# Seven products of half blocks in place of eight in the feed-forward's second projection

## The chip, the cores and the metric

The kernel runs on one core of one Trainium2 chip. The core has a matrix engine (TensorE, PE in the profile, with its weight loads shown apart as PEld), a vector engine (DVE), a scalar engine (ACT), a general engine (POOL) and a sync engine (SP) that here issues the loads. Working memory is SBUF, with 128 partitions; PE writes its sums to PSUM, which has eight banks of 128 x 512 floats. The metric is the time of one execution on the device, in microseconds (us); lower is better.

## The reference

A two-layer encoder over 512 tokens of 1024 features. Each layer mixes tokens (differential attention beside a bidirectional gated recurrence), projects the result and adds it to x, and then has a gated feed-forward with 2816 hidden features, which is the part that matters here:

```python
h = rmsnorm(x, ffn_norm[layer])
x = x + (jax.nn.silu(h @ w_gate[layer]) * (h @ w_up[layer])) @ w_down[layer]
```

All arrays are float32. `w_gate` and `w_up` are 1024 x 2816 for each layer. After the second layer comes one more normalisation.

## The kernel before

**Layout.** Activations are kept with features on the partitions: `xT` has 8 chunks of 128 features by 512 tokens. `hh` and `hl` are the two parts of `xT` times the gain of the norm: `hh` is the value rounded to the type that PE multiplies at full rate (fp32r), `hl` the rest. The norm's factor per token, `rbc`, is multiplied in after the projection, when a result leaves PSUM.

**A product in three matmuls.** Weights are split in the same way (`wsplit`, L196, by `split_act`, L91: ACT casts the high part, DVE subtracts it to get the low part), and `mm3` (L207) multiplies high by high, high by low, and low by high into one sum. One tile of 128 hidden features is 8 chunks x 3 matmuls of 128 x 128 weights by 512 tokens.

**The feed-forward loop** (L838 to L859). The 22 tiles of hidden features go in 11 pairs. For each pair one load each brings 1024 x 256 weights of `w_gate` and of `w_up` into a raw buffer (`wload`, L188; pool `wraw`, two buffers, issued on the SP queue). For each of the two tiles the gate's half of the columns is split and multiplied, then the up's half. The gate's sum is multiplied by `rbc` on DVE and goes through Silu on ACT; the up's sum is multiplied by `rbc`; their product is split into `gh` and `gl` (22 tiles by 512 tokens each), the operands of the projection by `w_down` that follows.

**Buffers.** Split weights have three pairs of buffers (`wsplit`, each 1024 elements of high part and of low part on a partition). Sums use four banks (`mbank`), and four more (`bank`) serve other work. Results in progress (`gu`) have two buffers for the gate and two for the up.

**Order.** The kernel is written in a tile framework that gives each engine its own list of instructions in order and puts the waits in. Work under `urgent()` goes ahead of other work that is ready at the same time: the loads, the splits, and all that takes a sum out of PSUM. Matmuls have normal priority and keep the order of the program as far as their operands are ready. A buffer is given to the next tile when all readers of the one in it are done.

Of the kernel before, what the change touches and what calls it, by code (L numbers as in the profile page):

```python
# [9 lines left out]
F32 = mybir.dt.float32  # L10
F32R = mybir.dt.float32r
I32 = mybir.dt.int32
I8 = mybir.dt.int8
AF = mybir.ActivationFunctionType
ALU = mybir.AluOpType
# [3 lines left out]
P = 128  # L19
D = 1024  # L20
DC = D // P
T = 512
# [4 lines left out]
FC = FFN // P  # L27
# [20 lines left out]
def kernel(  # L48
# [17 lines left out]
    PE, DVE, ACT, POOL = nc.tensor, nc.vector, nc.scalar, nc.gpsimd  # L66
    load = nc.sync.dma_start
    urgent = tc.high_priority

    def act(o, i, func, bias=None, scale=None, accum=None):  # L70
        kw = {}
        if bias is not None:
            kw["bias"] = bias
        if scale is not None:
            kw["scale"] = scale
        if accum is not None:
            kw["accum_out"] = accum
        return ACT.activation(o, i, func, **kw)  # L78

    def tt(o, a, b, op):  # L80
        return DVE.tensor_tensor(o, a, b, op)  # L81

    def stt(o, a, s, b, op0, op1):
        return DVE.scalar_tensor_tensor(o, a, s, b, op0, op1)
# [6 lines left out]
    def split_act(src, hi, lo):  # L91
        return ACT.copy(hi, src), tt(lo, src, hi.bitcast(F32), ALU.subtract)  # L92
# [9 lines left out]
    hp = ctx.enter_context(tc.tile_pool(name="wsplit", bufs=3))  # L102
# [4 lines left out]
    def bank(name="s"):  # L107
        return pside.tile([P, T], F32, tag="s", name=name)

    def mbank(name="m"):  # L110
        return pm.tile([P, T], F32, tag="m", name=name)
# [31 lines left out]
    xT = cp.tile([P, DC, T], F32, name="xT")  # L143
    hh = cp.tile([P, DC, T], F32R, tag="hh", name="hh")
    hl = cp.tile([P, DC, T], F32R, tag="hl", name="hl")
    rbc = cp.tile([P, T], F32, name="rbc")
# [41 lines left out]
    def wload(src):  # L188

        _, k, c = src.shape  # L190
        raw = wp.tile([P, 2048], F32, tag="raw", name="raw")
        v = raw[:, :k * c].rearrange("p (k c) -> p k c", c=c)
        load(v, src)
        return v

    def wsplit(v):  # L196

        _, k, c = v.shape
        hi = hp.tile([P, 1024], F32R, tag="hi", name="hi")[:, :k * c].rearrange("p (k c) -> p k c", c=c)
        lo = hp.tile([P, 1024], F32R, tag="lo", name="lo")[:, :k * c].rearrange("p (k c) -> p k c", c=c)  # L200
        split_act(v, hi, lo)
        return hi, lo

    def rows(w, k0, nk, c0, n):
        return w[k0 * P:(k0 + nk) * P, c0:c0 + n].rearrange("(k p) c -> p k c", p=P)

    def mm3(ps, lh, ll, rh, rl, start, stop):  # L207
        PE.matmul(ps, lh, rh, start=start, stop=False)  # L208
        PE.matmul(ps, lh, rl, start=False, stop=False)  # L209
        PE.matmul(ps, ll, rh, start=False, stop=stop)  # L210
# [44 lines left out]
    for j in range(5):  # L255
        b = 1 << j
        m = masks[:, j, :]
# [10 lines left out]
    with tc.tile_pool(name="init", bufs=1, reuse_waits="tile") as ip:  # L268
# [4 lines left out]
        with urgent():  # L273
            ACT.dma_start(vecs, small)
            for c in range(DC):
                if c % 4 == 0:
                    raw = wp.tile([P, 2048], F32, tag="raw", name="raw").rearrange("p (k d c) -> p k d c", k=4, d=2)
                src = w_in[0][c * P:(c + 1) * P, B_FF:B_FF + 2 * 512].rearrange("p (d c) -> p d c", d=2)[:, :, 0:2 * P]
# [7 lines left out]
        first = [mbank(), mbank(), bank("m"), bank("m")]  # L286
        for c in range(DC):
            with urgent():
                if c % 2 == 0:
                    hi, lo = [hp.tile([P, 1024], F32R, tag=tag, name=tag).rearrange("p (k d c) -> p k d c", k=2, d=2)  # L290
                              for tag in ("hi", "lo")]
                wh, wl = hi[:, c % 2], lo[:, c % 2]
# [17 lines left out]
        with tc.issue_after(norms[-1][1].ins):  # L310
# [53 lines left out]
            for dst, quarter in ((sin, 0.0), (cos, 0.25)):  # L364
                n = ip.tile([P, 32], F32, tag="n", name="n")
# [361 lines left out]
    last_silu = None  # L727
    for l in range(LAYERS):
        win = w_in[l]
        an = [vecs[:, V_FFN + 8 * l + c:V_FFN + 8 * l + c + 1] for c in range(DC)]  # L730
        with ExitStack() as mix:
# [59 lines left out]
            with tc.tile_pool(name=f"merge{l}", bufs=1, reuse_waits="tile") as gm, ExitStack() as late:  # L791
# [11 lines left out]
                with tc.tile_pool(name=f"attn{l}", bufs=1, reuse_waits="tile") as ap:  # L803
# [6 lines left out]
                               k=4, ah=obh, al=obl)  # L810
# [24 lines left out]
        with tc.tile_pool(name=f"ffn{l}", bufs=2, reuse_waits="tile") as fp:  # L835
            gh = fp.tile([P, FC, T], F32R, name="gh", bufs=1)
            gl = fp.tile([P, FC, T], F32R, name="gl", bufs=1)
            for f0 in range(0, FC, 2):  # L838
                with urgent():
                    rg = wload(rows(w_gate[l], 0, DC, f0 * P, 256))  # L840
                    ru = wload(rows(w_up[l], 0, DC, f0 * P, 256))
                for f in (f0, f0 + 1):
                    c0 = slice((f - f0) * P, (f - f0 + 1) * P)
                    tmp = []
                    for raw in (rg, ru):
                        with urgent():
                            wh, wl = wsplit(raw[:, :, c0])
                        ps = mbank()
                        for c in range(DC):
                            mm3(ps, wh[:, c, :], wl[:, c, :], hh[:, c, :], hl[:, c, :], c == 0, c == DC - 1)  # L850
                        s = fp.tile([P, T], F32, tag=f"gu{len(tmp)}", name="gu")
                        with urgent():
                            tt(s, ps, rbc, ALU.mult)
                            if not tmp:
                                last_silu = act(s, s, AF.Silu)
                        tmp.append(s)
                    with urgent():
                        tt(tmp[0], tmp[0], tmp[1], ALU.mult)
                        split_act(tmp[0], gh[:, f, :], gl[:, f, :])  # L859
            with tc.issue_after(last_silu.ins):  # L860
                lnexp = ACT.preload_act_table_set("natural_log_exp_and_others")
            groups = [(0, 8), (8, 8), (16, 6)]
            if l < LAYERS - 1:
                nn = [vecs[:, V_ATT + 8 * (l + 1) + c:V_ATT + 8 * (l + 1) + c + 1] for c in range(DC)]
                for c0 in range(0, DC, 2):
                    ps = [mbank(), mbank()]
                    for k0, nk in groups:
                        with urgent():
                            raw = wload(rows(w_down[l], k0, nk, c0 * P, 256))
                        for j in range(2):  # L870
                            with urgent():
                                wh, wl = wsplit(raw[:, :, j * P:(j + 1) * P])
                            for k in range(nk):
                                f = k0 + k
# [8 lines left out]
            else:  # L883
# [10 lines left out]
                ps = [[mbank(), mbank()] if t < 2 else [bank(), bank()] for t in range(TC)]  # L894
# [5 lines left out]
                for k, t, c0, n in order:  # L900
                    if k not in sp:
                        with urgent():
                            if k % 2 == 0:
                                raw = wload(rows(w_down[l], k, 2, 0, D))
                            sp[k] = wsplit(raw[:, k % 2:k % 2 + 1, :])
                    wh, wl = sp[k]
# [3 lines left out]
                for t in range(TC):  # L910
                    last = t == TC - 1
                    ss = sm.tile([P, 4], F32, tag="fss", name="fss")
                    v = [xt[:, t, c0:c0 + n] for c0, n in pieces[t]]
# [58 lines left out]
```

## Time and profile before

| | us |
|---|---|
| median of 3 runs | 1620.51 |
| lowest, highest | 1620.45, 1620.62 |
| the profiled execution | 1621.18 |
| its span, first to last instruction | 1619.2 |
| gate and up projections of layer 0, about | 452.3 to 691.2 |
| gate and up projections of layer 1, about | 1252 to 1491 |

In rows of groups the columns are the line of the kernel, the engine, the operation, out<-in by the program's names (`m` is a main bank, `s` a side bank), shapes, count, busy time, mean duration in ns, and the idle time of the engine before, with what ended it. In a timeline the first two numbers are start and duration. In rows by stage come the stretch, its length, then busy time and count of PE, weight loads, DVE, ACT and POOL, the granted clock of PE, the DMA share and GB/s. Durations of matmuls overlap, since they are pipelined and their ends are modelled, so the cost of one is read from the step between starts.

### The profile page before, as it was taken

Reading aid. Unit: us, or ns where it says so; the run is one execution under the profiler, and the core shown is the slowest. Engines: PE = TensorE matmul, PEld = TensorE weight load, DVE = VectorE, ACT = ScalarE, POOL = GpSimd, SP = SyncE. Lnnn points to the kernel's source line nnn. Section 1 sums busy time; section 2 is a strip of 40 time slices with the busy share of each in tenths; the row PEclk is TensorE's granted clock in tenths of the full one; section 3 lists DMA queues with packets and bytes.
Section 4 is the critical chain, followed back from the end, with each engine's and each line's share of the span. In section 5 each row is a group of like instructions: output and inputs, shape, how many; then the busy total and the mean of one; then the engine's idle time right before and its main releaser. Section 6 shows DMA issues by size and latency. Waiting matters only on the chain.

```text
span 1619.2 us, 18754 instructions
## 1 busy us (share of the span) xinstructions
PE 1604.5 (99%) x7473; PEld 1325.0 (82%) x7473; DVE 1013.5 (63%) x1637; ACT 772.0 (48%) x1188; POOL 9.1 (1%) x21
## 2 busy tenths in 40 slices
PE   9999999999999999999999999999999999999998
PEld 7888888887888888888888888888878888888886
DVE  8888877887654444433368789688875444444224
ACT  4666666676433323322355667676754323233213
POOL 2000000000000000000000000000000000000000
PEclk9999999999999999999999999999999999999999
DMA  6212212221333222323322222122123233332321
GB/s 206 88 58 73 79 57 75 78 79 53 104 104 98 85 87 95 114 90 100 102 91 83 74 78 79 54 77 79 52 79 100 83 104 104 105 103 93 104 82 74
DMA packets 118071, 142.53 MB, mean 88 GB/s; under 512 B 3168, under 2 KB 100704, under 8 KB 117984
## 3 DMA queue, kind: packets, MB, share of 16 engines
q1 hardware_dynamic: 117696, 141.05, 26.7%
q8 instruction: 58, 0.95, 0.2%
q10 hardware_dynamic: 288, 0.30, 0.1%
q14 instruction: 29, 0.24, 0.0%
HBM read 139.23 MB, written 2.10 MB: 87 GB/s over the span
## 4 chain that ended last, share of the span: by engine, by line
PE 85%; DVE 9%; ACT 4%; issue 1%; DMA 0%; SPq 0%; DVEq 0%; ACTq 0%
PE m L209 24%; PE m L210 24%; PE m L208 24%; DVE fl L81 2%; DVE lo L81 2%; PE sc L549 1%; PE s L208 1%; PE s L209 1%; PE s L210 1%; PE qk L666 1%; ACT hi L92 1%; DVE z L81 1%; PE wt L718 1%; PE po L600 1%; PE qk L663 1%
## 5 line engine op out<-in xcount | busy, mean ns | idle before, releaser
L92 ACT CAST hi<-raw 128x1024 fp32r<-128x1024 f32 (+2 forms) x274 | 272.4, 995 | 610.0 <-PE m L209 477.5
L208 PE MATMUL m<-hh,hi 128*128 128x512 f32 x1216 | 475.1, 391 | 0.9 <-ACT hh L78 0.5
L210 PE MATMUL m<-hh,lo 128*128 128x512 f32 x1216 | 475.4, 391 | 0.0
L209 PE MATMUL m<-hl,hi 128*128 128x512 f32 x1216 | 474.7, 390 | 0.0
L81 DVE TENSOR_TENSOR lo<-raw,hi 128x1024 fp32r<-128x1024 f32 (+2 forms) x282 | 321.0, 1139 | 182.7 <-ACT hi L92 181.8
L208 PEld LDWEIGHTS m<-hh,hi 128*128 128x128 f32 x1216 | 228.3, 188 | 47.9 <-ACT hh L78 1.0
L210 PEld LDWEIGHTS m<-hh,lo 128*128 128x128 f32 x1216 | 228.3, 188 | 47.6 <-DVE lo L81 0.7
L209 PEld LDWEIGHTS m<-hl,hi 128*128 128x128 f32 x1216 | 228.4, 188 | 47.0
L81 DVE TENSOR_TENSOR gu<-m,rbc 128x512 f32<-128x512 f32 x88 | 60.9, 692 | 241.3 <-PE m L210 237.3
L208 PE MATMUL m<-hi,hh 128*128 128x512 f32 x256 | 101.4, 396 | 0.0
L209 PE MATMUL m<-lo,hh 128*128 128x512 f32 x256 | 100.8, 394 | 0.0
L210 PE MATMUL m<-hi,hl 128*128 128x512 f32 x256 | 100.8, 394 | 0.0
L78 ACT ACTIVATE fl<-fl 128x1024 f32<-128x1024 f32 (+1 forms) x56 | 48.5, 873 | 44.8 <-DVE fl L81 44.8
L208 PE MATMUL m<-gh,hi 128*128 128x512 f32 x176 | 68.5, 389 | 0.0
L209 PE MATMUL m<-gl,hi 128*128 128x512 f32 x176 | 68.5, 389 | 0.0
L210 PE MATMUL m<-gh,lo 128*128 128x512 f32 x176 | 68.5, 389 | 0.0
L210 PEld LDWEIGHTS m<-hi,hl 128*128 128x128 f32 x256 | 48.1, 188 | 9.5
L209 PEld LDWEIGHTS m<-lo,hh 128*128 128x128 f32 x256 | 48.2, 188 | 9.3
L208 PEld LDWEIGHTS m<-hi,hh 128*128 128x128 f32 x256 | 48.2, 188 | 9.3
L549 PEld LDWEIGHTS sc<-fl 128*128 128x128 f32 x384 | 49.1, 191 | 7.9 <-issue 3.2
L549 PE MATMUL sc<-fl 128*128 128x128 f32 x384 | 51.3, 276 | 2.3 <-DVE fl L81 2.2
L208 PE MATMUL m<-mh,hi 128*128 128x512 f32 x128 | 49.4, 391 | 1.0 <-ACT hi L92 1.0
(258 smaller groups left out, 2353.9 us busy)
## 6 DMA issues: line engine op xcount, KB each, us to landing
raw<-in_w_in_dram SPq DMA_DIRECT2D x46, 1024.0 KB, 5.0
raw<-in_w_gate_dram SPq DMA_DIRECT2D x22, 1024.0 KB, 5.1
raw<-in_w_up_dram SPq DMA_DIRECT2D x22, 1024.0 KB, 5.1
raw<-in_w_down_dram SPq DMA_DIRECT2D x19, 1024.0 KB, 4.8
raw<-in_w_o_dram SPq DMA_DIRECT2D x8, 1024.0 KB, 4.7
raw<-in_w_b_dram SPq DMA_DIRECT2D x4, 1024.0 KB, 4.9
raw<-in_w_a_dram SPq DMA_DIRECT2D x4, 1024.0 KB, 5.0
raw<-in_w_down_dram SPq DMA_DIRECT2D x4, 768.0 KB, 4.1
```

Source lines behind the costliest of these rows:

```text
L78: return ACT.activation(o, i, func, **kw)
L81: return DVE.tensor_tensor(o, a, b, op)
L92: return ACT.copy(hi, src), tt(lo, src, hi.bitcast(F32), ALU.subtract)
L208: PE.matmul(ps, lh, rh, start=start, stop=False)
L209: PE.matmul(ps, lh, rl, start=False, stop=False)
L210: PE.matmul(ps, ll, rh, start=False, stop=stop)
L549: mm = PE.matmul(ps[:, c], K[:, c], Q[:, c], start=True, stop=True)
L600: mm = PE.matmul(po[:, tok], a, b, start=i == 0, stop=i == len(terms) - 1)
L663: mm = PE.matmul(ps[c], q2[:, c, tok], ka[:, c, :], start=True, stop=False)
L666: PE.matmul(ps[c], q2[:, c, tok], kb[:, c, :], start=False, stop=True)
L718: tr = PE.transpose(pt[:, s * P:(s + 1) * P], w[:, 0, s * P:(s + 1) * P], ident)
```

## The change

For the seven pairs of tiles 4 to 17 the up projection of a pair is computed as one 2 x 2 block product. The weights of the pair are cut into blocks by tile (i) and by even and odd chunks of the 1024 input features (j), a_ij; the activations by even and odd chunks and by halves of the tokens, x_jh. The usual way needs eight products of blocks; the new one (Winograd's form of Strassen's scheme) needs seven, of sums and differences of blocks. Each product is 4 chunks x 3 matmuls of 128 x 128 weights by 256 tokens. Gate tiles stay as they were, and so do the pairs of tiles 0 to 3 and 18 to 21, apart from the shape of their buffers.

- `combine(k)` makes the four mixed copies of the activations once for each layer, for one pair of chunks at a time: with the norm's gains, x12 - x11, x22 - x12 + x11, x22 - x12, and x21 - x22 + x12 - x11, each split into two parts. Four calls stand among the first four tiles. Two of the copies lie in the part of `gh` and `gl` for the last four tiles, which isn't filled until the end, and two in new tiles (`own`).
- `seven(rg, ru, f0)` makes the sums of weight blocks on DVE (two scratch tiles, and in place in the raw buffer), splits them into four sets of split buffers (`first` to `fourth`), runs the products between the two gate tiles, and puts the results together on DVE from three side banks and one main bank. `rbc` is multiplied into the gates' results, which are then multiplied with the ups', for both tiles in one instruction each.
- The results of a pair are now one tile of 2 x 512 for the gates and one for the ups, with a single buffer each.

```diff
         with tc.tile_pool(name=f"ffn{l}", bufs=2, reuse_waits="tile") as fp:
             gh = fp.tile([P, FC, T], F32R, name="gh", bufs=1)
             gl = fp.tile([P, FC, T], F32R, name="gl", bufs=1)
+            own = [fp.tile([P, DC // 2, 2, T // 2], F32R, name=name, bufs=1) for name in ("comh", "coml")]
+            half = lambda v: v.rearrange("p (h t) -> p h t", h=2)
+            spare = [v[:, FC - 4:FC, :].rearrange("p k (h t) -> p k h t", h=2) for v in (gh, gl)]
+            com = lambda part, i, k: (spare if i < 2 else own)[part][:, k, i % 2, :]
+
+            def combine(k):
+                ge, go = an[2 * k], an[2 * k + 1]
+                (x11, x12), (x21, x22) = [[half(xT[:, c, :])[:, i, :] for i in range(2)] for c in (2 * k, 2 * k + 1)]
+                d, e = [half(fp.tile([P, T], F32, tag=tag, name="com", bufs=1)) for tag in ("s1", "s2")]
+                u, v, m, n = d[:, 0, :], d[:, 1, :], e[:, 0, :], e[:, 1, :]
+                tt(u, x12, x11, ALU.subtract)
+                act(u, u, AF.Copy, scale=ge)
+                stt(m, x22, go, u, ALU.mult, ALU.subtract)
+                act(v, x12, AF.Copy, scale=ge)
+                stt(v, x22, go, v, ALU.mult, ALU.subtract)
+                stt(n, x21, go, m, ALU.mult, ALU.subtract)
+                for i, src in enumerate((u, m, v, n)):
+                    split_act(src, com(0, i, k), com(1, i, k))
+
+            def pair_of(tag):
+                return fp.tile([P, 2, T], F32, tag=tag, name="gu", bufs=1)
...
+            def gate(s, raw):
+                ps = tile_of(raw)
+                with urgent():
+                    tt(s, ps, rbc, ALU.mult)
+                    return act(s, s, AF.Silu)
+
+            def seven(rg, ru, f0):
+                s, u = pair_of("gu0"), pair_of("gu1")
+                quarter = u.rearrange("p f (h t) -> p (f h) t", h=2)
+                blk = lambda i, j: ru.rearrange("p (k two) c -> p k two c", two=2)[:, :, j, i * P:(i + 1) * P]
+                a11, a12, a21, a22 = blk(0, 0), blk(0, 1), blk(1, 0), blk(1, 1)
...
+                gate(s[:, 0, :], rg[:, :, 0:P])
+                with urgent():
+                    first = wsplit(ru[:, :, 0:P])
+                    second = two()
+                    tt(s1, a21, a22, ALU.add)
+                    tt(s2, s1, a11, ALU.subtract)
+                    split_act(s2, second[0][:, 0], second[1][:, 0])
+                    tt(a21, a11, a21, ALU.subtract)
+                    split_act(a21, second[0][:, 1], second[1][:, 1])
+                p1 = mbank()[:, :T // 2]
+                b26, b57, b34 = [half(bank("y")) for _ in range(3)]
+                product(p1, lambda part, k: first[part][:, 2 * k, :], plain(0, 0))
+                with urgent():
+                    ACT.copy(quarter[:, 1, :], p1)
+                product(b26[:, 0, :], lambda part, k: first[part][:, 2 * k + 1, :], plain(1, 0))
+                with urgent():
+                    third = two()
+                    split_act(s1, third[0][:, 0], third[1][:, 0])
+                    split_act(a22, third[0][:, 1], third[1][:, 1])
+                product(b26[:, 1, :], of(second, 0), mixed(1))
+                with urgent():
+                    tt(quarter[:, 0::3, :], quarter[:, 1:2, :].to_broadcast([P, 2, T // 2]), b26, ALU.add)
+                    tt(s2, a12, s2, ALU.subtract)
+                    fourth = two()
+                    split_act(s2, fourth[0][:, 0], fourth[1][:, 0])
+                product(b57[:, 1, :], of(second, 1), mixed(2))
+                product(b57[:, 0, :], of(third, 0), mixed(0))
+                with urgent():
+                    tt(quarter[:, 1:3, :], quarter[:, 3:4, :].to_broadcast([P, 2, T // 2]), b57, ALU.add)
+                    tt(quarter[:, 3, :], quarter[:, 2, :], b57[:, 0, :], ALU.add)
+                product(b34[:, 1, :], of(third, 1), mixed(3))
+                product(b34[:, 0, :], of(fourth, 0), plain(1, 1))
+                with urgent():
+                    tt(quarter[:, 1:3, :], quarter[:, 1:3, :], b34, ALU.add)
+                silu = gate(s[:, 1, :], rg[:, :, P:2 * P])
+                with urgent():
+                    tt(s, s, rbc.unsqueeze(1).to_broadcast([P, 2, T]), ALU.mult)
+                    tt(u, u, s, ALU.mult)
+                    split_act(u, gh[:, f0:f0 + 2, :], gl[:, f0:f0 + 2, :])
+                return silu
+
             for f0 in range(0, FC, 2):
                 with urgent():
                     rg = wload(rows(w_gate[l], 0, DC, f0 * P, 256))
                     ru = wload(rows(w_up[l], 0, DC, f0 * P, 256))
...
+                if 4 <= f0 < FC - 4:
+                    last_silu = seven(rg, ru, f0)
+                    continue
+                s, u = pair_of("gu0"), pair_of("gu1")
+                for i in range(2):
+                    if f0 + i < DC // 2:
+                        combine(f0 + i)
+                    last_silu = gate(s[:, i, :], rg[:, :, i * P:(i + 1) * P])
+                    ps = tile_of(ru[:, :, i * P:(i + 1) * P])
...
```

More of the change, by code (lines that the diff above doesn't have):

```diff
@@ new lines, in pair_of, with tile_of @@
+            def pair_of(tag):
+                return fp.tile([P, 2, T], F32, tag=tag, name="gu", bufs=1)
+            def tile_of(raw):
+                with urgent():
+                    wh, wl = wsplit(raw)
+                ps = mbank()
+                for c in range(DC):
+                    mm3(ps, wh[:, c, :], wl[:, c, :], hh[:, c, :], hl[:, c, :], c == 0, c == DC - 1)
+                return ps
+            def gate(s, raw):
[3 more added lines that the diff above has]
+                    return act(s, s, AF.Silu)
@@ new lines, in seven, with two, product @@
+            def seven(rg, ru, f0):
[3 more added lines that the diff above has]
+                a11, a12, a21, a22 = blk(0, 0), blk(0, 1), blk(1, 0), blk(1, 1)
+                s1, s2 = [fp.tile([P, T], F32, tag=tag, name="sw", bufs=1).rearrange("p (k c) -> p k c", c=P)
+                          for tag in ("s1", "s2")]
+                def two():
+                    return [hp.tile([P, 1024], F32R, tag=tag, name=tag).rearrange("p (h k c) -> p h k c", h=2, c=P)
+                            for tag in ("hi", "lo")]
+                def product(ps, w, right):
+                    for k in range(DC // 2):
+                        mm3(ps, w(0, k), w(1, k), right(0, k), right(1, k), k == 0, k == DC // 2 - 1)
+                plain = lambda odd, h: lambda part, k: half((hh, hl)[part][:, 2 * k + odd, :])[:, h, :]
+                mixed = lambda i: lambda part, k: com(part, i, k)
+                of = lambda v, h: lambda part, k: v[part][:, h, k, :]
+                gate(s[:, 0, :], rg[:, :, 0:P])
[33 more added lines that the diff above has]
+                silu = gate(s[:, 1, :], rg[:, :, P:2 * P])
+                with urgent():
+                    tt(s, s, rbc.unsqueeze(1).to_broadcast([P, 2, T]), ALU.mult)
+                    tt(u, u, s, ALU.mult)
+                    split_act(u, gh[:, f0:f0 + 2, :], gl[:, f0:f0 + 2, :])
+                return silu
@@ L841 @@
                     ru = wload(rows(w_up[l], 0, DC, f0 * P, 256))
[L842 to L856, printed above, removed]
+                if 4 <= f0 < FC - 4:
[7 more added lines that the diff above has]
+                    ps = tile_of(ru[:, :, i * P:(i + 1) * P])
                     with urgent():
-                        tt(tmp[0], tmp[0], tmp[1], ALU.mult)
-                        split_act(tmp[0], gh[:, f, :], gl[:, f, :])
+                        tt(u[:, i, :], ps, rbc, ALU.mult)
+                        tt(u[:, i, :], u[:, i, :], s[:, i, :], ALU.mult)
+                        split_act(u[:, i, :], gh[:, f0 + i, :], gl[:, f0 + i, :])
             with tc.issue_after(last_silu.ins):
```

## The prediction

> **What bounds the kernel now.** I read the page's busy shares and chain of waits first, then the busy times by stage, then inside the stage that the change touches the groups and the timeline.
>
> ```profile
> span 1619.2 us, 18754 instructions
> PE 1604.5 (99%) x7473; PEld 1325.0 (82%) x7473; DVE 1013.5 (63%) x1637; ACT 772.0 (48%) x1188; POOL 9.1 (1%) x21
> ...
> PE 85%; DVE 9%; ACT 4%; issue 1%; DMA 0%; SPq 0%; DVEq 0%; ACTq 0%
> ```
>
> TensorE is busy all through and carries 85% of the chain that ended last. By stage (length, then busy times of PE, weight loads, DVE, ACT):
>
> ```profile
> 0.00:446.00 446.00, 439.75 (x2123) 362.25 (x2124) 361.06 (x680) 276.09 (x455) 9.08 (x21) 1.00 0.26 86
> 452.30:495.82 43.52, 43.51 (x192) 35.56 (x192) 20.39 (x25) 16.09 (x20) 0.00 (x0) 1.00 0.30 96
> 495.82:691.20 195.38, 195.38 (x864) 161.83 (x863) 90.23 (x108) 60.26 (x73) 0.00 (x0) 1.00 0.32 101
> 1252.00:1491.00 239.00, 238.99 (x1066) 197.77 (x1065) 110.47 (x133) 77.18 (x95) 0.00 (x0) 1.00 0.32 103
> ```
>
> The second and third rows are the gate and up projections of layer 0 (first two pairs of feature tiles, then the other nine), the last those of layer 1. PE is without a gap in them, at clock 1.00, with DVE at 46% and ACT at 32%: here time is the number of matmuls by their spacing, and nothing else.
>
> The spacing comes from starts in the timeline, since the durations of matmuls overlap:
>
> ```profile
> 469.73 0.39 PE L208 MATMUL m<-hh,hi 128*128 128x512 f32 x1
> ...
> 475.17 0.39 PE L208 MATMUL m<-hh,hi 128*128 128x512 f32 x1
> ...
> 1610.41 0.28 PE L208 MATMUL s<-hi,gh 128*128 128x256 f32 x1
> ...
> 1612.44 0.28 PE L210 MATMUL s<-hi,gl 128*128 128x256 f32 x1
> ```
>
> The first two rows are 24 matmuls apart, one tile of 128 features: 5.44 us, 0.2267 us for each 512 columns. The last two stand at the ends of the kernel's only 18 matmuls of 256 columns (the last tile of tokens): 17 steps in 2.03 us, 0.1194 us each. So half the columns cost 0.527 of the time, not half.
>
> **The change, part by part.**
>
> *Products on PE.* For a pair of feature tiles the two up tiles take 2 x 8 x 3 = 48 matmuls of 512 columns: 48 x 0.2267 = 10.88 us. The new form has seven products of 4 chunks x 3 matmuls, 84 of 256 columns: 84 x 0.1194 = 10.03 us. With both gate tiles a pair goes from 21.76 to 20.91 us: 0.85 us less, of which eight-to-seven would give 1.36 and the dearer half width takes 0.51 back. Seven pairs in two layers: 14 x 0.85 = **11.9 us**. The start times are read to 0.01 us, so the spacing is good to about 0.0012 us, or 1.4 us in the sum.
>
> Each half-width matmul brings a full weight load, whose record is longer than the new spacing:
>
> ```profile
> L210 PEld LDWEIGHTS s<-hi,gl 128*128 128x128 f32 x5 | 1.0, 192 | 0.0
> ```
>
> Since each of the 18 matmuls had its own load, loads too came every 0.119 us; the 0.192 us is latency that overlaps. The Trainium skill, "TensorE: Matmul & The Clock Gate", "What overlaps and what doesn't", says that a load overlaps a running matmul only when it goes to another row group. By that, and with its figure of about 107 ns for 128 columns, a half-width step would be an estimated 0.107 + 0.107 = 0.21 us, and the 84 matmuls would take 17.9 us in place of 10.88. The trace disagrees: full-array loads came 0.119 us apart.
>
> *Work on DVE and ACT.* The rows for the pieces (columns: busy us, mean ns, idle before):
>
> ```profile
> L81 DVE TENSOR_TENSOR lo<-raw,hi 128x1024 fp32r<-128x1024 f32 x44 | 53.8, 1222 | 4.8 <-ACT hi L92 4.8
> L92 ACT CAST hi<-raw 128x1024 fp32r<-128x1024 f32 x44 | 46.4, 1054 | 146.8 <-PE m L209 144.2 <-issue 2.5
> L81 DVE TENSOR_TENSOR gu<-m,rbc 128x512 f32<-128x512 f32 x44 | 30.4, 692 | 120.8 <-PE m L210 118.8 <-ACT rbc L78 2.0
> L78 ACT ACTIVATE gu<-gu 128x512 f32<-128x512 f32 x22 | 13.9, 634 | 0.0
> L92 ACT CAST gh<-gu 128x512 fp32r<-128x512 f32 x22 | 13.7, 625 | 14.2 <-DVE gu L81 14.2
> ...
> L81 DVE TENSOR_TENSOR xt<-xt,s 128x256 f32<-128x256 f32 x2 | 0.8, 417 | 0.7 <-PE s L210 0.7
> L78 ACT ACTIVATE sqf<-xt 128x256 f32<-128x256 f32 x2 | 0.8, 409 | 0.8 <-DVE xt L81 0.8
> L84 DVE SCALAR_TENSOR_TENSOR xt<-xt,fss,fng 128x256 f32<-128x256 f32 x2 | 0.9, 480 | 0.6 <-ACT fss L78 0.6
> ```
>
> Before, a pair costs DVE 4 x 1.22 (low parts of weights) + 8 x 0.69 (evacuations, products, low parts of results) = 10.4 us. After: six operations of 1024 elements (three low parts of whole tiles, the scaling of both gates, the product, the low part of the result), fourteen of 512 (two gate evacuations, four sums of weight blocks, five low parts of them, three evacuations) and one of 256: 6 x 1.22 + 14 x 0.69 + 0.42 = **17.4 us of 20.91**, 83%. ACT goes to 4 x 1.05 + 5 x 0.62 + 2 x 0.63 + 0.41 = 9.0 us. Strided weight blocks I take at the same price, since the present split reads 128 of every 256 columns already. All of this lies beside PE as long as it is in time; without that cover it would be 7 us of DVE per pair.
>
> *Is it in time?* Count from the start of a pair's first gate tile. PE does that gate until 5.44, products 1 to 7 until 6.87, 8.30, 9.74, 11.17, 12.60, 14.04 and 15.47, the second gate until 20.91. There are three buffers of split weights, taken in turn by gate, first, second, third, fourth, gate. The third is free at 5.44 and wanted at 11.17, the fourth free at 8.30 and wanted at 14.04, the second gate free at 11.17 and wanted at 15.47, the next pair's gate free at 14.04 and wanted at 20.91, its first product free at 15.47 and wanted at 26.35, its second free at 20.91 and wanted at 29.2. A split takes 0.62 + 0.69 us (a block) or 1.05 + 1.22 us (a tile), so the tightest place, the second gate, has 4.30 us for 2.3. The end of a pair (0.69 + 0.63 + 1.22 + 1.22 + 1.05 + 1.22, with gaps some 7 us after 20.91) frees the single pair of result buffers at about 28; the next pair wants the gate one at 26.35 (free at about 25) and the other at 27.8. A delay there holds ACT or DVE, not PE, since the gates and the first product turn through four main banks and the other products through four side banks.
>
> *What is left on PE.* No stretch of before has this pattern. Bounds: nothing, as in the present stage; or as in the first row by stage, where DVE is at 81% as here and PE idles 446.00 - 439.75 = 6.25 us: scaled to 14 x 20.91 = 293 us, 4.1 us. The waits of that stage are mostly for operands just computed, and hardly for split weights:
>
> ```profile
> PE sc L549 <- DVE fl L81: 2.2, 4, 1.1
> ...
> PE m L208 <- ACT hi L92: 1.0, 2, 0.5
> ```
>
> so I take 2.0 us, the middle.
>
> *The four mixed copies of the activations.* Each of four calls of combine in a layer has 3 x 0.48 + 5 x 0.42 = 3.5 us of DVE and 6 x 0.41 = 2.5 us of ACT, at default priority behind the urgent work, in the first two pairs: DVE 20.4 + 14 of 43.5 us. PE hides it; uncovered it would be 28 us in two layers, which I exclude because splits run a whole tile (5.44 us) ahead there. The larger pair buffers, the unchanged last two pairs, and the bytes loaded cost nothing: the loads are the same two of 1 MB per pair on the SP queue.
>
> **Sum.** 1621.18 (the profiled execution; its span 1619.2) - 11.9 + 2.0 = 1611.3; the median is 0.67 below the profiled one, so **1610.6 us**. This case by itself spans 1607.2 (no wait, spacing at its lower error) to 1612.7 (4.1 us of waits).
>
> **Rivals.**
>
> *A raw buffer comes too late (slower).* There are two buffers of raw weights, and the loads hang on the splits:
>
> ```profile
> SPq L193 <- DVE lo L81: 1431.4, 123, 35.7
> ...
> 472.69 1.22 DVE L81 TENSOR_TENSOR lo<-raw,hi 128x1024 fp32r<-128x1024 f32 x1
> ...
> 473.94 0.37 SPq L193 DMA_DIRECT2D raw<-in_w_gate_dram  x1
> ...
> raw<-in_w_gate_dram SPq DMA_DIRECT2D x22, 1024.0 KB, 5.1
> ```
>
> If the next pair's gate weights have to wait for this pair's gate buffer, whose second half is split only from 11.17 on: 11.2 + 1.05 + 1.22 + 5.1 (landing) + 1.05 + 1.22 and gaps gives 21.0, against 21.36 when the third matmul of the next gate wants the low part. Slack 0.4 us. Two DVE operations in front (0.69 + 1.22) make it 1.5 us late per pair: 1608.6 + 14 x 1.5 = **1629.6**. It decides from 0.85 us of lateness per pair, 1.25 us of DVE delay in that chain. Against it: the up buffer is last read by the third and fourth splits, at about 8 to 11 us, so it is free first, and a load into it lands by 16.3, over 2 us before it is wanted.
>
> *Splits late by one DVE operation.* DVE is in order at 83%, and an evacuation that waits for PE holds what stands behind it. One operation of 0.69 to 1.22 us in front of the chain above, less its 0.4 us, costs 0.3 to 0.8 us per pair: 1612.8 to **1619.8**. For it: DVE idles 118.8 us before gu in layer 0 now and will have little left. Against it: windows of 2 us or more beyond the split time at every other buffer.
>
> *No gain.* If a long run of half-width matmuls goes at 10.88 / 84 = 0.1295 us instead of 0.1194, the change does no less PE work: **1620.5**. The 18 matmuls are a short run; but loads and matmuls kept their step to the last of them.
>
> *Weight loads bind.* If in a long run loads can't overlap each other and cost their record of 0.192 us each, a pair's products take 16.1 us: 1608.6 + 14 x 6.10 = **1694**. The 18 steps of 0.119 us speak against it. The skill's rule above lies on this side too, at an estimated 1608.6 + 14 x 7.9 = 1719.
>
> **How the numbers follow.** Forecast 0.62; splits late 0.18; raw buffer late 0.13; no gain 0.05; weight loads 0.02. The range takes in the first two, 1607.0 to 1619.8. A measurement of this kernel tells about 0.2% (3.2 us) from no change: faster than 1617.3 are the forecast and two thirds of the second case, 0.74; the same are the rest of that and no gain, 0.11; slower 0.15.
>
> **What would show it.** In the changed profile: half-width matmuls 0.119 us apart through a whole product, and over product boundaries; pairs 20.9 us apart; DVE near 17.4 us in each; PE waits in that stage under 0.3 us per pair. A gate load that follows the low part of the second gate half, with PE waiting once per pair for hi or lo of a gate, would show the raw buffer; waits at products 3 to 7 would show DVE. I am wrong if the spacing is over 0.125 us, or if PE stands for 0.4 us or more in each pair.

## The result, and the profile after

| | before, us | after, us |
|---|---|---|
| median | 1620.48 (4 runs) | 1610.49 (4 runs, 1609.58 to 1612.3) |
| ratio, 95% interval | | 0.994 (0.9923 to 0.9957) |
| the same kernels in a second series | 1620.92 | 1609.86 (5 runs), ratio 0.9931 (0.9919 to 0.9944) |
| profiled execution, its span | 1621.18, 1619.2 | 1612.3, 1610.6 |

The change saves 10 to 11 us, 0.6 to 0.7%, and neither interval reaches 1. The profile page of the changed kernel, busy shares and chain:

```profile
span 1610.6 us, 20117 instructions
PE 1595.3 (99%) x7977; PEld 1342.1 (83%) x7977; DVE 1122.2 (70%) x1827; ACT 814.2 (51%) x1292; POOL 8.0 (0%) x21
...
PE 85%; DVE 9%; ACT 4%; issue 1%; DMA 1%; SPq 0%; DVEq 0%; ACTq 0%
```

PE still binds, with 504 matmuls more and 9 us less of busy time; DVE gained 109 us of work. The row by stage for the seven pairs of layer 0 (stretch, length, busy PE, weight loads, DVE, ACT):

```profile
495.50:641.80 146.30, 146.30 (x923) 133.16 (x922) 109.47 (x143) 58.14 (x83) 0.00 (x0) 1.00 0.32 101
```

Seven pairs in 146.3 us are 20.9 us each, PE is without a gap, and DVE is busy 109.47 / 7 = 15.6 us in each, 75%. The waits of PE in the whole kernel name no operand of these pairs. Those on split weights (`hi`, from ACT in two places and from DVE at L296 in the first projection) were there before, the last with 0.4 us:

```profile
PE st L502 <- ACT kt L497: 2.1, 1, 2.1
PE sc L549 <- DVE fl L81: 1.8, 3, 1.1
PE idle L266 <- DVE ones_r L119: 1.4, 1, 1.4
PE m L208 <- DVE hi L296: 1.1, 1, 1.1
PE m L208 <- ACT hi L92: 1.0, 2, 0.5
```

In the timeline, the seven products of the second pair begin with the first of these rows and end where the next gate tile begins, with the second:

```profile
521.92 0.28 PE L208 MATMUL m<-hh,hi 128*128 128x256 f32 x1
...
531.99 0.40 PE L208 MATMUL m<-hh,hi 128*128 128x512 f32 x1
532.23 0.40 PE L209 MATMUL m<-hl,hi 128*128 128x512 f32 x1
```

84 matmuls in 10.07 us: 0.1199 us each, through all six boundaries between products. The products of the other 13 pairs take 10.07 or 10.08 us as well, so PE waits nowhere in them.

**Where the time went.** The stage runs from the first matmul on `hh` (a row of the timeline) to the first on `gh` (the first of the two start times in its group's row). Before, then after:

```profile
448.50 0.39 PE L208 MATMUL m<-hh,hi 128*128 128x512 f32 x1
...
L208 PE MATMUL m<-gh,hi x176: 389/389/389, 688.7 to 807.7; 128*128 128x512 f32 x176
```

```profile
451.29 0.39 PE L208 MATMUL m<-hh,hi 128*128 128x512 f32 x1
...
L208 PE MATMUL m<-gh,hi x176: 389/389/389, 685.9 to 804.9; 128*128 128x512 f32 x176
```

240.2 against 234.6 us: 5.6 less, 0.80 per pair. Layer 1, from the same kind of rows (its end is the first transposition of `xT`), goes from 1248.49 to 1488.67 and from 1245.44 to 1480.01: 240.2 against 234.6 again. The two stages together save 11.2 us. (These rows put the stages some 3 us earlier than the rounded 452.3 to 691.2 and 1252 to 1491 ahead of the prediction.) Of the 11.2 us the profiled execution gave 2.8 back ahead of the first stage, 451.29 against 448.50, in code that is the same in both kernels.

### The profile page after: what moved, and what is told of

It reads as the page before. It is cut to its first block, busy times and chain, and to the rows that moved or that the text cites. A ratio compares the mean times of both kernels' runs of the same rounds, so it can differ in the third digit from the quotient of the medians.

```text
span 1610.6 us, 20117 instructions
## 1 busy us (share of the span) xinstructions
PE 1595.3 (99%) x7977; PEld 1342.1 (83%) x7977; DVE 1122.2 (70%) x1827; ACT 814.2 (51%) x1292; POOL 8.0 (0%) x21
## 4 chain that ended last, share of the span: by engine, by line
PE 85%; DVE 9%; ACT 4%; issue 1%; DMA 1%; SPq 0%; DVEq 0%; ACTq 0%
PE m L209 21%; PE m L210 21%; PE m L208 21%; PE y L210 3%; PE y L209 3%; PE y L208 3%; DVE lo L81 2%; PE sc L549 2%; DVE fl L81 2%; PE s L209 1%; PE s L208 1%; PE s L210 1%; PE qk L666 1%; ACT hi L92 1%; DVE z L81 1%
## 5 line engine op out<-in xcount | busy, mean ns | idle before, releaser
L208 PE MATMUL m<-hh,hi 128*128 128x512 f32 (+1 forms) x1048 | 404.4, 386 | 1.2 <-DVE hi L296 1.1
L210 PE MATMUL m<-hh,lo 128*128 128x512 f32 (+1 forms) x1048 | 403.9, 386 | 0.0
L209 PE MATMUL m<-hl,hi 128*128 128x512 f32 (+1 forms) x1048 | 403.6, 385 | 0.0
L208 PEld LDWEIGHTS m<-hh,hi 128*128 128x128 f32 x1048 | 197.5, 189 | 40.2 <-ACT sq L78 1.5
L210 PEld LDWEIGHTS m<-hh,lo 128*128 128x128 f32 x1048 | 197.0, 188 | 38.4 <-DVE lo L81 0.2
L209 PEld LDWEIGHTS m<-hl,hi 128*128 128x128 f32 x1048 | 197.1, 188 | 38.0
L81 DVE TENSOR_TENSOR gu<-m,rbc 128x512 f32<-128x512 f32 x60 | 41.3, 689 | 61.7 <-PE m L210 60.6
L92 ACT CAST gh<-gu 128x512 fp32r<-128x512 f32 (+1 forms) x30 | 24.7, 822 | 56.6 <-DVE gu L81 56.5
```

## Experiments

**The changed kernel again.** No edit.

> The changed kernel once more. Theory: the feed-forward stages are 5.6 to 5.7 us shorter each in every execution (no PE wait in them), and what varies between runs lies ahead of the first feed-forward, in code that both kernels share. Then this trace shows the first gate matmul at 448.5 to 451.5 us, the first matmul of w_down 234.6 us behind it, and a time of 1609.5 to 1612.5 us. Rival: the 2.8 us lost ahead of the first feed-forward belong to the change; then the first gate matmul stands at 451 us again and no run is under 1609.5 us.

1609.86 us median (1609.63 to 1610.96), and in its trace:

```profile
449.06 0.39 PE L208 MATMUL m<-hh,hi 128*128 128x512 f32 x1
...
L208 PE MATMUL m<-gh,hi x176: 389/389/389, 683.6 to 802.6; 128*128 128x512 f32 x176
```

The stage lasts 234.5 us as before; its start came back from 451.29 to 449.06. So the stage is what the change set, and the 2.8 us ahead of it belonged to that execution. In the ten traces of variants below, this start lies between 448.2 and 448.7. Most of the difference between the two executions has a visible place. PE waits for the same operand in both; soon behind it the granted clock (the third number from the end in a row by stage) is 0.50 in the first execution and 1.00 in this one:

```profile
77.42 2.03 PE L502 MATMUL st<-vB,kt 128*128 128x128 f32 x12 [2.09 <-ACT kt L497]
...
79.00:80.00 1.00, 1.00 (x7) 1.00 (x6) 1.00 (x2) 0.00 (x0) 0.00 (x0) 0.50 0.00 0
```

```profile
76.26 1.60 PE L502 MATMUL st<-vB,kt 128*128 128x128 f32 x12 [1.83 <-ACT kt L497]
...
79.00:80.00 1.00, 1.00 (x6) 0.80 (x6) 1.00 (x5) 0.39 (x1) 0.00 (x0) 1.00 0.08 16
```

The low clock lasts 3.4 us, and the same matmuls take 1.6 us longer with it, of the 2.2 us that separate the two starts. Why it came in one execution only isn't shown.

**Half width alone.** The kernel before, its 48 up matmuls of 512 columns in the 14 pairs cut into 96 of 256:

```diff
-                        for c in range(DC):
-                            mm3(ps, wh[:, c, :], wl[:, c, :], hh[:, c, :], hl[:, c, :], c == 0, c == DC - 1)
+                        halves = [(0, 256), (256, 256)] if tmp and 4 <= f0 < FC - 4 else [(0, T)]
+                        for t0, n in halves:
+                            for c in range(DC):
+                                mm3(ps[:, t0:t0 + n], wh[:, c, :], wl[:, c, :], hh[:, c, t0:t0 + n], hl[:, c, t0:t0 + n],
+                                    c == 0, c == DC - 1)
```

> The kernel before, with the up tiles of the same 14 pairs computed as two halves of 256 tokens each: the usual eight products, 96 matmuls of 256 columns for a pair in place of 48 of 512, and no sums of blocks. Theory (half-width matmuls cost 0.120 us each, and PE sets the time): 96 x 0.120 - 10.88 = 0.64 us more per pair, 14 x 0.64 = 9 us, 1629.5 us. Rival (the dearer half width is hidden, or a start-up share of each group is what costs): 1620.5 us, or more than 1634 us.

1630.31 us, ratio 1.0056 (1.0043 to 1.007): 9.4 us more, 0.67 per pair. The dearer half width is real and not hidden. Seven of eight products take 12 x 0.12 = 1.44 us from that: -1.44 + 0.67 = -0.77 per pair, near the -0.80 of the stages.

**Quarter width.** The same edit with four parts of 128 tokens.

> The kernel before, with the up tiles of the same 14 pairs in four parts of 128 tokens: 192 matmuls of 128 columns for a pair in place of 48 of 512. If a matmul costs a fixed 0.013 us and its columns (0.2267 for 512, 0.1199 for 256), 128 columns cost 0.067 us, a pair's up tiles 12.8 us in place of 10.88, and the time is 1620.9 + 14 x 1.9 = 1648 us. Rival (weight loads bind: half width was just above what a load takes, some 0.11 us): 192 x 0.11 = 21.1 us, 1620.9 + 14 x 10.2 = 1764 us.

1770.24 us, ratio 1.092 (1.0903 to 1.0936): the rival. Two rows of its timeline, 36 matmuls apart:

```profile
519.88 0.28 PE L208 MATMUL m<-hh,hi 128*128 128x128 f32 x1
...
523.90 0.28 PE L208 MATMUL m<-hh,hi 128*128 128x128 f32 x1
```

4.02 / 36 = 0.112 us for 128 columns, hardly less than the 0.120 for 256. So something other than the columns sets the step at 128. The Trainium skill, "TensorE: Matmul & The Clock Gate", "LDWEIGHTS (loading the stationary operand)", gives columns / 1.2 GHz for a load, whatever the rows, which is an estimated 107 ns for 128; the step of 112 ns lies 5% above it. The same page's "Back-to-back issue gap" has about 81 ns for a sustained stream of loads and 128-column matmuls; here it was 112 ns. Load and narrow matmul were not separated, since every matmul here has a load of its own (7977 of each in the changed kernel).

**Raw buffers in turn.**

```diff
+    turn = [0]
+
     def wload(src):
...
-        raw = wp.tile([P, 2048], F32, tag="raw", name="raw")
+        raw = wp.tile([P, 2048], F32, tag=f"raw{turn[0] % 2}", name="raw", bufs=1)
+        turn[0] += 1
```

This holds for every load that `wload` makes; the one other place that takes raw buffers, in the first projection, gets the same two names.

> The changed kernel with the two raw buffers taken strictly in turn, so that the next pair's gate weights must wait until this pair's gate buffer is split. Theory of the raw buffer (11.2 + 1.05 + 1.22 + 5.1 + 1.05 + 1.22 us against 21.36, slack 0.4 us, one DVE operation in front of it costs 0.3 to 0.8 us): the gate load is issued about 13.6 us into a pair, PE waits once per pair at the gate's low part, 0.3 to 1.5 us, 1614 to 1631 us. Rival (the order of splits shifts so that the gate half is split early, and the slack holds): within 1 us of the changed kernel, 1610.5 us.

1610.52 us (1610.33 to 1612.31): no loss to speak of, so the expected 0.3 to 1.5 us per pair was wrong. The chain itself is as drawn, and so is its slack. In the first pair, which starts at 492.70 (24 matmuls of full width ahead of the first half-width one, at 498.14):

```profile
506.31 0.37 SPq L196 DMA_DIRECT2D raw<-in_w_gate_dram  x1
...
511.34 2.00 ACT L92 CAST hi<-raw 128x1024 fp32r<-128x1024 f32 x2 [6.32 <-DMA raw<-in_w_gate_dram]
...
512.43 2.36 DVE L81 TENSOR_TENSOR lo<-raw,hi 128x1024 fp32r<-128x1024 f32 x2 [2.73 <-ACT hi L92]
...
514.13 0.39 PE L213 MATMUL m<-hh,lo 128*128 128x512 f32 x1
```

The gate load goes out 13.6 us into the pair, the cast waits 6.32 us for it, the low part of the first half is done half way through the two of 2.36 us, at about 513.6, and the matmul that wants it starts at 514.13. Half a microsecond was enough; DVE had been idle for 2.73 us when the split came. One pair of the 14 waited, for 0.5 us. What a DVE operation in front would cost wasn't run.

**More DVE work.** The first sum of weight blocks written 4, 8 or 12 times more per pair, with no change of the result (5, 9 or 13 in the loop):

```diff
-                    tt(s1, a21, a22, ALU.add)
+                    for _ in range(5):
+                        tt(s1, a21, a22, ALU.add)
```

> The changed kernel with the first sum of weight blocks (s1) written four more times in each of the 14 pairs, which changes no result: 4 x 0.61 = 2.4 us more of DVE per pair, 15.6 + 2.4 = 18.0 of 20.9 us. Theory (DVE has slack, PE sets the time): the stage stays at 234.6 us, the time at 1609.9 us. Rival (splits late by one DVE operation): PE waits 0.3 us or more per pair, 1614 us or more.

> The same with eight more: 15.6 + 4.9 = 20.5 of 20.9 us of DVE per pair, 98%. Theory: the cover is nearly gone; waits begin, 0 to 0.5 us per pair, 1610 to 1617 us. Rival (splits late): 0.5 to 1.5 us per pair, 1617 to 1631 us.

> The same with twelve more: 15.6 + 7.3 = 22.9 us of DVE per pair, more than PE's 20.9. Theory (DVE takes over when its own sum passes PE's): a pair lasts about 22.9 to 23.5 us, 28 to 36 us more in all, 1638 to 1646 us. Rival (the order of DVE matters more than its sum): 1650 us or more.

1654.85, 1675.56 and 1701.15 us; ratios 1.021 (1.0189 to 1.0231), 1.0337 (1.0319 to 1.0354) and 1.0492 (1.0476 to 1.0508). My theory fell at the first of them: 2.4 us more of DVE cost 45 us (1654.85 against 1609.86), some 3.2 per pair; the second is outside both of its ranges, and the third is where its rival put it. But by the row of the first, DVE isn't full, and PE stands:

```profile
495.50:641.80 146.30, 132.85 (x830) 120.02 (x829) 112.13 (x150) 51.46 (x76) 0.00 (x0) 1.00 0.27 87
```

DVE is busy 112.13 of 146.3 us, 77%. The wait has one place, in 12 of the 14 pairs (waits of PE, then DVE and ACT and PE in the timeline of one pair):

```profile
PE y L208 <- ACT hi L92: 32.0, 12, 2.8
...
524.00 0.68 DVE L81 TENSOR_TENSOR gu<-gu,y 128x512 f32<-128x512 f32 x1
524.60 0.69 DVE L81 TENSOR_TENSOR raw<-raw 128x512 f32<-128x512 f32 x1
...
525.32 0.62 ACT L92 CAST hi<-raw 128x512 fp32r<-128x512 f32 x1 [1.43 <-DVE raw L81]
...
525.99 0.38 PE L208 MATMUL y<-comh,hi 128*128 128x256 f32 x1 [2.34 <-ACT hi L92]
```

`raw<-raw` is the subtraction a11 - a21, whose split is the operand of the fourth product in order. It stands behind `gu<-gu,y`, the evacuation that has to wait for the product just ahead on PE, the third in order (product 6 of the scheme). So the operand is begun when PE already wants it. In the changed kernel the same two stand the other way round and 9 us apart:

```profile
516.99 0.68 DVE L81 TENSOR_TENSOR raw<-raw 128x512 f32<-128x512 f32 x1
...
526.43 0.69 DVE L81 TENSOR_TENSOR gu<-gu,y 128x512 f32<-128x512 f32 x1
```

The listed waits make 32.0 of the 45 us. Most of the rest is the clock of PE. From the first half-width matmul to the next of full width, the seven products last 10.07 us in the changed kernel. In this run they last that in the first pair of each layer, 12.7 to 13.2 us in seven pairs, and 14.0 to 14.8 us in the other five, where the granted clock falls to 0.50 for 3.4 us behind the wait:

```profile
646.23 0.39 PE L208 MATMUL y<-comh,hi 128*128 128x256 f32 x1 [2.81 <-ACT hi L92]
...
648.65 0.41 PE L208 MATMUL y<-gh,hi 128*128 128x256 f32 x1
...
650.78 0.41 PE L209 MATMUL y<-gl,hi 128*128 128x256 f32 x1
...
648.00:651.00 3.00, 3.00 (x16) 3.00 (x16) 1.23 (x1) 1.04 (x1) 0.00 (x0) 0.50 1.00 306
```

The second and third row are ten matmuls apart: 0.213 us each in place of 0.120. The five pairs lose 1.4 us more than the seven on average, 7 us in all. With twelve more sums such a spell, of 3.4 or 6.8 us, begins in each of the 12 waits, which are now some 5 us long; the pairs lose 6.9 to 8.2 us each, 90 in all, of which the listed waits are 60.8.

New theory: the order of DVE starts the loss, not its sum. Two runs tell them apart.

**The same DVE work elsewhere.** Four more copies of that evacuation in place of the sums:

```diff
-                    tt(quarter[:, 0::3, :], quarter[:, 1:2, :].to_broadcast([P, 2, T // 2]), b26, ALU.add)
+                    for _ in range(5):
+                        tt(quarter[:, 0::3, :], quarter[:, 1:2, :].to_broadcast([P, 2, T // 2]), b26, ALU.add)
```

> The changed kernel with the same 2.4 us more of DVE per pair as dve4, but at another place: the evacuation of products 2 and 6 is written five times in place of once, which changes no result. Theory (dve4 lost 45 us because in its order of DVE the subtraction a11 - a21 stands behind the evacuation that waits for product 6, so that its split comes after the matmul that wants it; not because of the sum of DVE): here the subtraction stands early, PE waits nowhere, 1610 us within 2 us. Rival (2.4 us more of DVE are too much wherever they stand): 1640 us or more.

1609.65 us (1609.12 to 1609.71), ratio 0.9927 (0.9913 to 0.994): no cost at all, with as much DVE work added as in the run with four sums, and DVE at 126.69 / 146.3 = 87%:

```profile
495.50:641.80 146.30, 146.30 (x924) 133.13 (x923) 126.69 (x170) 58.65 (x83) 0.00 (x0) 1.00 0.31 101
```

**The four sums again, the subtraction ahead of s2.**

```diff
                     for _ in range(5):
                         tt(s1, a21, a22, ALU.add)
+                    tt(a21, a11, a21, ALU.subtract)
                     tt(s2, s1, a11, ALU.subtract)
                     split_act(s2, second[0][:, 0], second[1][:, 0])
-                    tt(a21, a11, a21, ALU.subtract)
                     split_act(a21, second[0][:, 1], second[1][:, 1])
```

> dve4 with the subtraction a11 - a21 moved in the program ahead of the difference s2: the same instructions, the same sum of DVE. Theory (order): the subtraction is issued before the evacuation, the wait of 2.7 us per pair for that split is gone, 1610 to 1615 us. Rival (sum): as dve4, 1655 us.

1619.47 us (10 runs, 1617.77 to 1622.1), ratio 0.9991 (0.9982 to 1.0): 35 of the 45 us come back by moving one line. The time is still above what I expected. In its waits the 12 at a split have become 2:

```profile
PE y L208 <- ACT hi L92: 3.5, 2, 1.8
...
PE y L210 <- DVE lo L81: 0.4, 2, 0.3
```

These 3.9 us are not the whole 9.6 that are left (1619.47 against 1609.86). By the length of the seven products, two pairs lose 3.9 and 2.4 us: each has a wait of about 1.8 us, and in the first the granted clock falls to 0.50 for 3.4 us behind it. In ten pairs the products last 0.24 to 0.51 us longer, 3.3 in all, because the first matmul of a product that wants a low part is late:

```profile
589.34 0.28 PE L209 MATMUL y<-coml,hi 128*128 128x256 f32 x1
589.76 0.39 PE L210 MATMUL y<-comh,lo 128*128 128x256 f32 x1
```

That is 0.42 us from start to start in place of 0.12. Most of these delays don't show among the waits of PE, since the record of a matmul lasts 0.28 us and covers the greater part of them. Together the 12 pairs lose 9.6 us. So the low parts, which DVE makes, are still a little late in this order.

**Eight and nine pairs.** The condition of the loop, and for nine all of `combine` in the first pair:

```diff
-                if 4 <= f0 < FC - 4:
+                if 2 <= f0 < FC - 2:
...
-                    if f0 + i < DC // 2:
-                        combine(f0 + i)
+                    if f0 == 0:
+                        combine(2 * i)
+                        combine(2 * i + 1)
```

> The changed kernel with an eighth pair in each layer (tiles 18 and 19) by seven products; the mixed copies that lie in gh and gl for tiles 18 to 21 are read for the last time in that pair, before its results are written. Theory (PE alone sets the time, 0.81 us per pair): 2 x 0.81 = 1.6 us less than the changed kernel, 1608.9 us. Rival (the results of that pair wait for the reads, and DVE at 83% is late into the last pair): no gain, 1610.5 us or more.

> Nine pairs per layer by seven products (tiles 2 to 19), with all four calls of combine in the first pair. Theory (0.81 us per pair as long as the splits keep their place): 4 x 0.81 = 3.2 us less than the changed kernel, 1606.7 us. Rival (combine's 11 to 14 us of DVE don't fit beside the first pair, and the mixed copies are late for the second): PE waits once per layer, 1 to 4 us, 1608 to 1615 us.

Eight (with `4 <= f0 < FC - 2` and `combine` as it was): 1608.4 us, ratio 0.992 (0.9907 to 0.9934). Nine: 1607.06 us, ratio 0.9914 (0.99 to 0.9927), and the waits of PE name no operand of the pairs. Each further pair in a layer brings 1.3 to 1.5 us over both layers; the intervals overlap each other and that of the changed kernel, but the stages show it directly. With nine:

```profile
448.64 0.39 PE L208 MATMUL m<-hh,hi 128*128 128x512 f32 x1
...
L208 PE MATMUL m<-gh,hi x176: 389/389/389, 681.7 to 800.7; 128*128 128x512 f32 x176
```

233.1 us, 1.5 less than the changed kernel for two more pairs. This is the fastest version that was run.

## Why the prediction was right

- **The gain on PE, 0.85 us per pair.** Right in kind, a little too large: 0.80. The step of half-width matmuls is 0.1199 us in a long run, not the 0.1194 read from 18 of them (0.04 us per pair), and the first matmuls of full width behind them start 0.23 to 0.24 us apart. In all 11.2 us in place of 11.9.
- **What is left on PE, 2.0 us.** This term was mis-sized: nothing is left in the stage. It was scaled from a stage with DVE 81% busy, but busy time isn't what makes such waits: at 87% (the added evacuations) PE waited nowhere, and at 77% (the four sums) it waited in 12 pairs.
- **The two errors and the variation between executions cancel.** Stages alone would give 1609.3 (1620.5 - 11.2); the two series had 1610.49 and 1609.86. That the forecast stood within 0.2 us of the first is partly luck.
- **DVE 17.4 us of 20.9.** Measured 15.6, because operations of 512 elements start 0.60 us apart where each lasts 0.69 (the rows at 524.00 and 524.60 above); I had added durations.
- **In time.** Right by the table of buffers: in the first pair, from 495.50, the next gate load went out 7.7 us in (predicted 8 to 11, from the up buffer) and the up load 13.6 us in, when the gate buffer is free (11.17 + 1.05 + 1.22 = 13.4 by the prediction's figures).
- **Mixed copies at no cost.** Right: no PE wait appears in the stage, even with all of them beside the first pair (nine pairs).
- **The raw buffer.** Chain and slack were right (0.4 us predicted, 0.5 measured when it was forced). The loss was to come from DVE operations in front of the split; in the forced run there were none.
- **Splits late by one operation.** The rival exists, but I had its place and its price wrong: not the gate's split at 0.3 to 0.8 us, but the second set's, at 3.2 us per pair when a subtraction falls behind an evacuation. The price has a part that the prediction left out, the lower clock behind a wait. The changed kernel is safe by its order of DVE, which I had assumed rather than checked, and not by slack in DVE's sum.
- **Weight loads bind.** Not at 256 columns, with 0.1199 us a step. At 128 columns the step of 0.112 us may be the load's.

## What to carry to other kernels

Before trading matmuls for narrower ones, measure the step at the new width: 512, 256 and 128 columns cost 0.227, 0.120 and 0.112 us here, so one product in eight was worth taking at half width. At a quarter, seven eighths of 192 matmuls would take an estimated 168 x 0.112 = 18.8 us in place of 10.88. Whether work beside a full PE is free depended here on its place more than on its amount: 17 us more on DVE in seven pairs cost nothing as evacuations, and as much ahead of one subtraction cost 3.2 us per pair. And a wait of PE can cost more than its length: behind five of twelve here the matmuls ran at half the clock for 3.4 us. So look in the queue of each engine for an operand that stands behind a wait for the matmul just ahead of its use, and move it ahead in the program.

## What the runs showed of the hardware

The cost of a narrow matmul isn't a fixed part plus its columns: from 512 and 256 columns one would expect 0.067 us for 128, and 0.112 was measured.

At some waits of PE the granted clock falls to 0.50 for 3.4 us, and with eight or twelve more sums also for 6.8 us. It does so behind one of the two waits of about 1.8 us (four sums, the subtraction moved), five of the twelve of up to 2.8 us (four sums), and in all twelve of some 5 us (twelve sums). Within a spell half-width matmuls start 0.213 us apart in place of 0.120. What decides it behind the shorter waits isn't shown.
